# ScalarE copies placed before VectorE subtractions, two intermediates moved to PSUM, and new bookings, in a one-core decoder layer

## The chip, the cores and the metric

The kernel runs on one core of one Trainium2 chip. The metric is the device time of one execution in microseconds (us). The core has a matmul engine (TensorE, PE in the profile, with its weight loads as PEld), VectorE (DVE), ScalarE (ACT), GpSimd (POOL) and SyncE (SP), which issues nearly all DMAs here. Each engine runs its own instructions strictly in the order of the program and waits on semaphores.

## What is computed

One decoder layer on 512 tokens of width 1024, in fp32. The core of it, cut from the reference:

```python
h = rms_norm(x, n1g) * (1 + sc1) + sh1            # sc1, sh1 ... from silu(c) @ ada_w
proj = h @ w_in                                   # 1024 x 3400
y_moba = moba_attention(qm, km, vm)               # 6 heads x 64
y_conv = conformer_conv(ca, cg, ...)              # 31 taps, 256 channels, layer norm, silu
score = sum_h wi[t,h] * relu(qi[t,h] . ki[s])     # indexer; causal; 8 heads x 64
y_dsa = attention over the top 128 keys by score  # 6 heads x 64
mix = [rms_norm(y_moba), y_conv, rms_norm(y_dsa)]
x = x + g1 * (mix @ w_out)
h2 = rms_norm(x, n2g) * (1 + sc2) + sh2
y = top-1 group of 4, top-2 of its 8 experts: (silu(h2 @ w1) * (h2 @ w3)) @ w2, gated
out = rms_norm(x + g2 * y, final_g)
```

## The kernel before

The program is one long list of instructions written in an order that the Python code fixes by hand; no scheduler reorders it. It has three parts.

First (0 to about 46 us of the profiled span) the condition vector is multiplied with `ada_w`, the first norm is made, and the indexer's projections are accumulated in five PSUM banks (`pidx`).

Second (to about 355 us) come the projections, the attention and the output projection. A loop over `ORDER` (L1088) takes eleven pairs of 128-column blocks ("units") of `w_in`. Each unit is eight steps of k; a step is three products of 512 columns (high x high, high x low, low x high halves of fp32 numbers, L468 to L470, or six of 256 columns for the value units, L463 to L465). Between the steps, other work is woven in:

- `finish` (L573) takes a finished unit out of its PSUM bank. For a query unit `stacked` (L621) copies one half of the partitions on ScalarE (L624) and subtracts on VectorE (L625), then does the same for the other half. For a key unit L599 to L601 do so with two copies per half. Instructions of two engines on one PSUM bank are held apart by semaphores.
- In the first three pairs, `idx_item` (L663) makes one head's indexer score at every second step: two products (L671, L672), a relu on ScalarE into a buffer `a` of which there are four (L674), and a multiply-add into `acc` on VectorE (L675). After the eighth head `topk` books the search for the 128th score: 16 times MAX8 and MATCH_REPLACE8 and a mask (L690, L693, L696), 33 steps for each of three query tiles.
- Such background work on VectorE stands in three lists `bg`, taken in their order. `spent` (L532) adds credit for planned matmul time times `RATE` (0.5 in the first three pairs, then 0.6) and releases the next booked item when the credit covers its price. `conv_taps` books 16 taps of the convolution on VectorE (L716) for each of two channel halves; 14 more go to ScalarE and GpSimd (L727, L728), one every third step.
- `after(n, f)` runs f n steps later. `att_item` (L815) makes one pair of heads for one query tile: scores (L631, L633), minimum and mask on VectorE (L828), exponentials on ScalarE (L830); then after `lag(0)` steps the scaling (L834 to L842), after `lag(1)` the transposes and their copies (L849, L851), after `lag(2)` the product with the values (L863, copy L868, squares L872 and L874), after `lag(3)` the sum of squares as a product (L882) and, once a group of tiles is complete, the root `rsqrt` (L258 to L263, eleven VectorE steps on 128x1 to 128x4 numbers) and, `L6` steps after it, `spread` (L335), which transposes the root for use by all columns. The lags are `L1` to `L4`, and `LT` after the loop over `ORDER`.
- `ada_load` (L942) and `ada_use` (L956) multiply the rest of `ada_w` in 1 MB pieces; the first `ada_load` also clears a row buffer on GpSimd (L937), and SyncE's small DMAs into that buffer (L939) wait for it, ahead of the piece's own DMA (L948).

The loop ends with `put`, which splits the mixed rows, and 40 steps of the output projection follow, with the last four attention items among them; then four tiles are finished and routed (`Tile2`, `route`).

Third (355 us to the end) come 16 blocks of two experts each, with 1 MB weight loads, and the final norm (`final_ops`, L1823). The change touches in it only `rsqrt_ops`.

Of the kernel before, what the change touches and what calls it, by code (L numbers as in the profile page):

```python
# [34 lines left out]
NG = 2  # L35
RATE = [0.5, 0.6]
EVERY = 4.25
L1 = 4
L2 = 4
L3 = 4  # L40
L4 = 6
L5 = 3
# [39 lines left out]
L6 = 3  # L82
LT = (3, 3, 3, 4)
NF = 2
VADA = (0, 0)
ORDER = [(0, 3), (9, 11), (10, 12), (1, 4), (6, 7), (2, 5), (13, 16), (8, 19), (14, 17), (20, 21), (15, 18)]


@with_exitstack
def tile_hybrid_layer(  # L90
# [25 lines left out]
    def mk(pool, shape, dt, tag, bufs):  # L116
        cnt[0] += 1
        return pool.tile(shape, dt, tag=tag, bufs=bufs, name=f"{tag}_{cnt[0]}")
# [134 lines left out]

    def rsqrt_ops(r, v, n, shape):

        b, t = mk(sm, [P, NT], F32, "rq", 8)[:, :shape[1]], mk(sm, [P, NT], F32, "rq", 8)[:, :shape[1]]
        ri = r.bitcast(I32)
        ops = [lambda: V.tensor_scalar(b, v, 1.0 / n, EPS, op0=OP.mult, op1=OP.add),  # L258
               lambda: V.tensor_scalar(ri, b.bitcast(I32), -0.5, float(0x5f3759df), op0=OP.mult, op1=OP.add)]
        for _ in range(3):  # L260
            ops += [lambda: V.scalar_tensor_tensor(t, r, -0.5, b, op0=OP.mult, op1=OP.mult),
                    lambda: V.tensor_tensor(t, t, r, op=OP.mult),
                    lambda: V.scalar_tensor_tensor(r, t, 1.5, r, op0=OP.add, op1=OP.mult)]  # L263
        return ops

    def rsqrt(r, v, n, shape):
        for f in rsqrt_ops(r, v, n, [P, r.shape[1]]):
            f()
# [14 lines left out]
    def first_norm():  # L283
# [17 lines left out]
        A.activation(sc, col("c", 0, 8), AF.Silu)  # L301
        rsqrt(rstd, ss, D, [P, NT])
        for k in range(2, TA):
# [247 lines left out]
    def after(n, f):  # L551
        later.append([n, f])
# [20 lines left out]
    def finish(u, p):  # L573
# [10 lines left out]
        else:  # L584
# [9 lines left out]
            if i == 0:  # L594
                stacked(d, p)
            else:
                kl = (tq if (m, j) in (("m", 1), ("d", 0)) else tb)([P, T], F32R)
                for e_, own, other in HALVES:
                    A.copy(d[e_][own], p[own])  # L599
                    A.copy(d[e_][other], p[own])  # L600
                    V.tensor_tensor(kl[own], p[own], d[e_][own].bitcast(F32), op=OP.subtract)  # L601
                d = d + [kl]
            after(LQ, lambda: qkv.__setitem__((m, u - b), d))

# [16 lines left out]
    def stacked(d, p):  # L621

        for e_, own, other in HALVES:
            A.copy(d[e_][own], p[own])  # L624
            V.tensor_tensor(d[e_][other], p[own], d[e_][own].bitcast(F32), op=OP.subtract)  # L625

# [36 lines left out]
    def idx_item(qt, h):  # L663
        n = (qt + 1) * P
        if h == 0:
# [6 lines left out]
        PE.matmul(p[:, :n], q, kl[:, :n], start=False, stop=True)  # L672
        r = ta([P, T])
        A.activation(r[:, :n], p[:, :n], AF.Relu)  # L674
        V.scalar_tensor_tensor(acc[:, :n], r[:, :n], wi[:, qt - 1, h:h + 1],  # L675
                               cmask[:, 384 - qt * P:] if h == 0 else acc[:, :n],
# [5 lines left out]
    def topk(qt):  # L682
        n = (qt + 1) * P
        acc = am[qt]
        d = n / 960 + 0.07
        m8 = [None]
# [21 lines left out]
    def conv_taps(j):  # L708
# [21 lines left out]
        def f2():  # L730
            while any(e[0] == j for e in taps):
                taps.pop(0)[1]()
            V.tensor_tensor(cy[j], cy[j], cz[j], op=OP.add)
        bg[2].append((0.4, f0))
        for w in range(30 - TAPS):
            bg[2].append((0.6, lambda w=w: f1(w)))
        if TAPS:
# [77 lines left out]
    def att_item(m, qt, j):  # L815
# [61 lines left out]
        def f4(sq):  # L877
# [5 lines left out]
            for g in GROUPS[m]:  # L883
                if qt in g and done[m].issuperset(g):
                    r = mk(sm, [P, NT], F32, "r4", 3)[:, :len(g)]
                    rsqrt(r, pss[m][:, g[0]:g[-1] + 1], 384, [P, NT])
                    after(L6, lambda r=r, g=g: f5(r, g))

# [1050 lines left out]
```

## Time and profile before

| | |
|---|---|
| median of 3 runs | 862.08 us (861.08 to 864.18) |
| the profiled execution | 859.55 us |
| its span in the trace | 857.7 us |
| PE busy | 812.6 us (95%) |
| VectorE busy | 460.0 us (54%) |
| ScalarE busy | 263.8 us (31%) |
| GpSimd busy | 267.0 us (31%) |
| granted clock of TensorE, mean | 0.984 |

Busy time is the union of an engine's instructions. A matmul's end is modelled, so a PE that is busy may still run below its pace. The granted clock is a share of 2.4 GHz; 0.5 is 1.2 GHz. In a timeline row the number in square brackets is the idle time of the engine before the instruction, with the one that released it. Times inside the span are counted from its start.

### The profile page before, as it was taken

Reading aid. Unit: us, or ns where it says so; the run is one execution under the profiler, and the core shown is the slowest. Engines: PE = TensorE matmul, PEld = TensorE weight load, DVE = VectorE, ACT = ScalarE, POOL = GpSimd, SP = SyncE. Lnnn points to the kernel's source line nnn. Section 1 sums busy time; section 2 is a strip of 40 time slices with the busy share of each in tenths; the row PEclk is TensorE's granted clock in tenths of the full one; section 3 lists DMA queues with packets and bytes.
Section 4 is the critical chain, followed back from the end, with each engine's and each line's share of the span. In section 5 each row is a group of like instructions: output and inputs, shape, how many; then the busy total and the mean of one; then the engine's idle time right before and its main releaser. Section 6 shows DMA issues by size and latency. Waiting matters only on the chain.

```text
span 857.7 us, 12505 instructions
## 1 busy us (share of the span) xinstructions
PE 812.6 (95%) x4669; PEld 481.1 (56%) x4669; DVE 460.0 (54%) x1054; ACT 263.8 (31%) x573; POOL 267.0 (31%) x314
## 2 busy tenths in 40 slices
PE   6999899998999889989999999999999999999992
PEld 4888576575676678434645446346436445454431
DVE  5779989899658856573233242152333232332425
ACT  5265467645567423341110101011101001101004
POOL 1463867665413640505005013031050050050002
PEclk9999899999999999999999999999999999999997
DMA  9970554273324646679799999999999999999922
GB/s 348 335 176 1 194 171 146 81 235 109 124 99 167 250 169 276 275 289 362 280 422 419 420 418 420 419 418 420 419 421 418 420 420 418 420 419 387 375 90 101
DMA packets 76233, 252.00 MB, mean 294 GB/s; under 512 B 7575, under 2 KB 40449, under 8 KB 51082
## 3 DMA queue, kind: packets, MB, share of 16 engines
q1 hardware_dynamic: 76106, 251.15, 75.7%
q8 instruction: 38, 0.62, 0.3%
q14 instruction: 25, 0.20, 0.1%
q10 hardware_dynamic: 64, 0.02, 0.0%
HBM read 249.05 MB, written 2.10 MB: 293 GB/s over the span
## 4 chain that ended last, share of the span: by engine, by line
PE 74%; DVE 16%; ACT 3%; issue 3%; DMA 1%; POOL 1%; SPq 1%; ACTq 0%; DVEq 0%; POOLq 0%
PE ps L1488 26%; PE ps L1522 13%; PE ps L1550 7%; PE ps L1586 6%; DVE q L716 4%; DVE b L693 2%; DVE sm L690 2%; DVE b L675 2%; PE ps L468 2%; DMA ad<-in_ada_w_dram 1%; PE ps L470 1%; PE ps L469 1%; PE ps L1070 1%; PE ps L1071 1%; PE ps L1072 1%
## 5 line engine op out<-in xcount | busy, mean ns | idle before, releaser
L1570 POOL TENSOR_SCALAR v<-c,sm 128x128 bf16<-128x128 f32 x112 | 65.1, 603 | 313.4 <-DVE sm L1601 313.4
L1488 PE MATMUL ps<-u,x 128*64 128x512 f32 x280 | 103.2, 594 | 0.0
L1542 DVE TENSOR_TENSOR q<-ps,q 128x512 f32<-128x512 f32 x118 | 72.7, 683 | 40.6 <-PE ps L1550 40.6
L346 POOL TENSOR_TENSOR u<-r,u 128x512 fp32r<-128x512 f32 x55 | 76.5, 1399 | 54.0 <-ACT u L345 46.4
L1505 DVE SCALAR_TENSOR_TENSOR a<-a,sm,ps 128x512 f32<-128x512 f32 x16 | 12.0, 748 | 129.6 <-PE ps L1488 87.5
L1488 PE MATMUL ps<-h,x 128*64 128x512 f32 x248 | 78.9, 594 | 0.0
L1488 PE MATMUL ps<-r,x 128*64 128x512 f32 x240 | 78.2, 594 | 0.0
L1522 PE MATMUL ps<-u,a 128*64 128x512 f32 x200 | 70.1, 614 | 2.5 <-ACT a L1514 2.5
L1532 DVE TENSOR_TENSOR ps<-ps,q 128x512 f32<-128x512 f32 (+1 forms) x33 | 22.4, 678 | 71.7 <-PE ps L1522 71.7
L1533 ACT CAST a<-ps 128x512 fp32r<-128x512 f32 (+1 forms) x33 | 18.9, 573 | 135.2 <-DVE ps L1532 135.2
L468 PE MATMUL ps<-h,u 128*128 128x512 f32 x128 | 54.6, 427 | 0.0
L1550 PE MATMUL ps<-a,v 128*128 128x512 f32 (+1 forms) x132 | 54.3, 413 | 0.0
L1488 PEld LDWEIGHTS ps<-u,x 128*64 128x64 f32 x280 | 31.4, 137 | 37.8 <-issue 35.8
L470 PE MATMUL ps<-h,u 128*128 128x512 f32 x128 | 51.5, 402 | 0.0
L469 PE MATMUL ps<-h,u 128*128 128x512 f32 x128 | 51.3, 401 | 0.0
L1522 PE MATMUL ps<-h,a 128*64 128x512 f32 (+1 forms) x144 | 50.5, 572 | 0.6 <-DVE g L1535 0.6
L1550 PE MATMUL ps<-g,v 128*128 128x512 f32 (+1 forms) x132 | 50.8, 387 | 0.1
L1488 PEld LDWEIGHTS ps<-r,x 128*64 128x64 f32 x240 | 24.0, 137 | 38.4 <-issue 35.8
L1522 PE MATMUL ps<-r,a 128*64 128x512 f32 x120 | 43.0, 596 | 0.0
L728 POOL TENSOR_TENSOR q<-q,g 128x510 f32<-128x510 f32 (+12 forms) x26 | 36.0, 1385 | 20.3 <-ACT g L727 13.1
L1594 ACT ACTIVATE x<-ps,c,c 128x256 f32<-128x256 f32 x28 | 14.3, 560 | 90.5 <-PE ps L1586 90.5
L1497 ACT ACTIVATE a<-ps 128x512 f32<-128x512 f32 x16 | 9.6, 598 | 104.6 <-PE ps L1488 93.5
(372 smaller groups left out, 1815.4 us busy)
## 6 DMA issues: line engine op xcount, KB each, us to landing
u<-in_expert_w_dram SPq DMA_DIRECT2D x60, 1024.0 KB
r<-in_expert_w_dram SPq DMA_DIRECT2D x48, 1024.0 KB
h<-in_expert_w_dram SPq DMA_DIRECT2D x46, 1024.0 KB
z<-in_expert_w_dram SPq DMA_DIRECT2D x24, 1024.0 KB
r<-in_ada_w_dram SPq DMA_DIRECT2D x16, 1024.0 KB
r<-in_w_in_dram SPq DMA_DIRECT2D x22, 512.0 KB
ad<-in_ada_w_dram SPq DMA_DIRECT2D x8, 1024.0 KB
h<-in_expert_w_dram SPq DMA_DIRECT2D x16, 256.0 KB
```

The costliest lines, as they stand in the source:

```text
L346: eng.tensor_tensor(l, r, h.bitcast(F32), op=OP.subtract)
L468: PE.matmul(p, wh, h, start=k == 0, stop=False)
L469: PE.matmul(p, wh, l, start=False, stop=False)
L470: PE.matmul(p, wl, h, start=False, stop=k == KD - 1)
L716: V.scalar_tensor_tensor(cy[j][:, s:], cu[j][:, :T - s], col("cw", 2 * w + j), cy[j][:, s:], op0=OP.mult, op1=OP.add)
L728: G.tensor_tensor(cz[j][:, s:], cz[j][:, s:], t[:, s:], op=OP.add)
L1488: PE.matmul(self.pu[s, :], self.feature(k)[:, s], self.w[i][e][k // 4][:, k % 4, :], start=k == 0, stop=k == KD - 1)
L1522: PE.matmul(self.py[nh][s, cs], self.hT[:, k, s], self.second(e, k, nh)[:, cs], start=k == 0, stop=k == 3)
L1542: V.tensor_tensor(xr[t_, nh], self.product(yy, t_), xr[t_, nh], op=OP.add)
L1550: PE.matmul(pc[:, cs] if held else pc, self.ot[:n, t_ * P:(t_ + 1) * P], yy[q][:n, cs], start=not held and q == 0, stop=last and q == 1)
L1570: ops.append(lambda o=b.choice(ch, t_), c_=c_[:, t_:t_ + 1]: eng.tensor_scalar(o, iota, c_, None, op0=OP.is_equal))
L1586: PE.matmul(p[:, kk], hb[q][t_][i][:, k * P:k * P + P], self.o[t_ // 2][:, t_ % 2], start=t_ == 0 and q == 0, stop=t_ == NT - 1 and q == 1)
```

## The change

In `finish` and `stacked`, ScalarE's copies of a bank are all issued first, and VectorE's subtractions follow. In `idx_item` the relu is written back into the PSUM bank and VectorE reads it there. In `rsqrt_ops` the two intermediates stand in a PSUM tile (except in the first norm). The price of a search step rises by 0.13 and that of a convolution tap from 0.6 to 0.95, the second `RATE` from 0.6 to 0.8. `L4` goes from 6 to 10, `LT` from (3, 3, 3, 4) to (2, 3, 2, 3), the wait before the moba group's spread from 3 to 6 steps, the wait before the last pair's heads may be used from 6 to 4, and the last pair is projected in the order 18, 15.

```diff
--- before.py
+++ after.py
@@ -33,12 +33,12 @@
 NA = 4
 NV = 5
 NG = 2
-RATE = [0.5, 0.6]
+RATE = [0.5, 0.8]
 EVERY = 4.25
 L1 = 4
 L2 = 4
 L3 = 4
-L4 = 6
+L4 = 10
 L5 = 3
 VSOON = 0
 PUT0 = 4
@@ -80,10 +80,10 @@
 WOL = ((-2, 1, 2), (-1, 0, 0), (-1, 0, 4))
 GROUPS = {"m": ((0, 1, 2, 3),), "d": ((0,), (1, 2, 3))}
 L6 = 3
-LT = (3, 3, 3, 4)
+LT = (2, 3, 2, 3)
 NF = 2
 VADA = (0, 0)
-ORDER = [(0, 3), (9, 11), (10, 12), (1, 4), (6, 7), (2, 5), (13, 16), (8, 19), (14, 17), (20, 21), (15, 18)]
+ORDER = [(0, 3), (9, 11), (10, 12), (1, 4), (6, 7), (2, 5), (13, 16), (8, 19), (14, 17), (20, 21), (18, 15)]
 
 
 @with_exitstack
@@ -251,9 +251,11 @@
             nc.sync.dma_start(rw[:, b, 0:4], router_group_w[0, i * T:(i + 1) * T].rearrange("(p k) e -> p k e", k=4))
             nc.sync.dma_start(rw[:, b, 8:40], router_expert_w[0, i * T:(i + 1) * T].rearrange("(p k) e -> p k e", k=4))
 
-    def rsqrt_ops(r, v, n, shape):
-
-        b, t = mk(sm, [P, NT], F32, "rq", 8)[:, :shape[1]], mk(sm, [P, NT], F32, "rq", 8)[:, :shape[1]]
+    def rsqrt_ops(r, v, n, shape, apart=True):
+
+
+        w = ps([P, 2, NT]) if apart else mk(sm, [P, 2, NT], F32, "rq", 8)
+        b, t = w[:, 0, :shape[1]], w[:, 1, :shape[1]]
         ri = r.bitcast(I32)
         ops = [lambda: V.tensor_scalar(b, v, 1.0 / n, EPS, op0=OP.mult, op1=OP.add),
                lambda: V.tensor_scalar(ri, b.bitcast(I32), -0.5, float(0x5f3759df), op0=OP.mult, op1=OP.add)]
@@ -263,8 +265,8 @@
                     lambda: V.scalar_tensor_tensor(r, t, 1.5, r, op0=OP.add, op1=OP.mult)]
         return ops
 
-    def rsqrt(r, v, n, shape):
-        for f in rsqrt_ops(r, v, n, [P, r.shape[1]]):
+    def rsqrt(r, v, n, shape, apart=True):
+        for f in rsqrt_ops(r, v, n, [P, r.shape[1]], apart):
             f()
 
     def turns(*chains):
@@ -299,7 +301,7 @@
         for k in range(2):
             A.copy(xk(k), pt[k])
         A.activation(sc, col("c", 0, 8), AF.Silu)
-        rsqrt(rstd, ss, D, [P, NT])
+        rsqrt(rstd, ss, D, [P, NT], False)
         for k in range(2, TA):
             A.copy(xk(k), pt[k])
         p = spread(rstd)
@@ -598,9 +600,10 @@
                 for e_, own, other in HALVES:
                     A.copy(d[e_][own], p[own])
                     A.copy(d[e_][other], p[own])
+                for e_, own, other in HALVES:
                     V.tensor_tensor(kl[own], p[own], d[e_][own].bitcast(F32), op=OP.subtract)
                 d = d + [kl]
-            after(LQ, lambda: qkv.__setitem__((m, u - b), d))
+            after(LQ - 2 if ci == NC - 1 else LQ, lambda: qkv.__setitem__((m, u - b), d))
 
     vals = {}
 
@@ -622,6 +625,7 @@
 
         for e_, own, other in HALVES:
             A.copy(d[e_][own], p[own])
+        for e_, own, other in HALVES:
             V.tensor_tensor(d[e_][other], p[own], d[e_][own].bitcast(F32), op=OP.subtract)
 
     def product_of_pair(p, q, qs, k, kl, n):
@@ -670,9 +674,8 @@
         q = qi[h // 2][h % 2][:, qt * P:(qt + 1) * P]
         PE.matmul(p[:, :n], q, kh[:, :n], start=True, stop=False)
         PE.matmul(p[:, :n], q, kl[:, :n], start=False, stop=True)
-        r = ta([P, T])
-        A.activation(r[:, :n], p[:, :n], AF.Relu)
-        V.scalar_tensor_tensor(acc[:, :n], r[:, :n], wi[:, qt - 1, h:h + 1],
+        A.activation(p[:, :n], p[:, :n], AF.Relu)
+        V.scalar_tensor_tensor(acc[:, :n], p[:, :n], wi[:, qt - 1, h:h + 1],
                                cmask[:, 384 - qt * P:] if h == 0 else acc[:, :n],
                                op0=OP.mult, op1=OP.add)
         spent(0.11 * (qt + 1))
@@ -682,7 +685,7 @@
     def topk(qt):
         n = (qt + 1) * P
         acc = am[qt]
-        d = n / 960 + 0.07
+        d = n / 960 + 0.2
         m8 = [None]
 
         def f1():
@@ -731,9 +734,9 @@
             while any(e[0] == j for e in taps):
                 taps.pop(0)[1]()
             V.tensor_tensor(cy[j], cy[j], cz[j], op=OP.add)
-        bg[2].append((0.4, f0))
+        bg[2].append((0.7, f0))
         for w in range(30 - TAPS):
-            bg[2].append((0.6, lambda w=w: f1(w)))
+            bg[2].append((0.95, lambda w=w: f1(w)))
         if TAPS:
             for w in range(29, 29 - TAPS, -1):
                 taps.append((j, lambda w=w: g1(w)))
@@ -884,7 +887,7 @@
                 if qt in g and done[m].issuperset(g):
                     r = mk(sm, [P, NT], F32, "r4", 3)[:, :len(g)]
                     rsqrt(r, pss[m][:, g[0]:g[-1] + 1], 384, [P, NT])
-                    after(L6, lambda r=r, g=g: f5(r, g))
+                    after(L6 + 3 * (m == "m"), lambda r=r, g=g: f5(r, g))
 
         def f5(r, tiles):
             q = spread(r)
```

## Rows read from the trace of the kernel before

**Rows 1.** Windows: length; busy us of PE, PEld, DVE, ACT, POOL; clock; DMA; GB/s.
```profile
85.80:107.20 21.40, 17.44 (x68) 12.53 (x67) 20.99 (x40) 10.69 (x20) 18.48 (x13) 0.84 0.57 194
...
193.00:214.40 21.40, 18.78 (x104) 12.10 (x107) 20.20 (x38) 11.33 (x30) 11.26 (x14) 0.92 0.33 109
...
300.20:321.60 21.40, 18.12 (x77) 14.98 (x78) 12.44 (x29) 5.31 (x11) 10.64 (x9) 0.92 0.47 169
...
643.30:686.20 42.90, 42.90 (x248) 22.24 (x246) 12.46 (x23) 4.99 (x9) 0.00 (x0) 1.00 1.01 420
```

**Rows 2.** Waits of PE from 40 to 420 us: total us, times, longest.
```profile
PE ps L335 <- DVE r L263: 5.0, 2, 4.3
PE ps L978 <- DMA r<-in_ada_w_dram: 4.0, 1, 4.0
PE ps L882 <- ACT q L868: 2.6, 1, 2.6
PE ps L863 <- ACT a L851: 2.5, 2, 1.4
...
PE ps L849 <- DVE v L838: 1.7, 3, 1.1
```

**Rows 3.** Timeline, 81 to 100 us, one engine after another: start, us, instruction.
```profile
81.54 0.67 DVE L582 TENSOR_TENSOR q<-q,a 128x512 f32<-128x512 f32 x1
...
82.25 0.72 ACT L724 ACTIVATE q<-q,m 128x511 f32<-128x511 f32 x1 [3.75 <-DVE q L582]
...
92.73 0.53 POOL L937 MEMSET q<- 128x512 f32 x1
...
94.52 0.36 SPq L948 DMA_DIRECT2D r<-in_ada_w_dram  x1
...
99.94 1.93 PE L978 MATMUL ps<-r,c 128*32 128x512 f32 x8 [3.96 <-DMA r<-in_ada_w_dram]
```

**Rows 4.** The indexer's multiply-add by its line: ns minimum/median/maximum, first and last start.
```profile
L675 DVE SCALAR_TENSOR_TENSOR b<-a,m,b x21: 483/740/1742, 57.9 to 102.2; 128x256 f32<-128x256 f32 x7, 128x384 f32<-128x384 f32 x7, 128x512 f32<-128x512 f32 x7
```

**Rows 5.** Timeline, 201 to 207 us, VectorE, ScalarE and PE.
```profile
201.38 3.90 DVE L716 SCALAR_TENSOR_TENSOR q<-q,m,q 128x485 f32<-128x485 f32 x4
...
206.03 0.58 ACT L624 CAST z<-ps 64x512 fp32r<-64x512 f32 x1 [2.63 <-DVE z L625]
...
203.73 0.40 PE L469 MATMUL ps<-h,u 128*128 128x512 f32 x1
203.97 0.40 PE L470 MATMUL ps<-h,u 128*128 128x512 f32 x1
206.95 0.38 PE L882 MATMUL ps<-c,a 128*128 128x1 f32 x2 [2.58 <-ACT q L868]
```

**Rows 6.** Timeline, 164 to 167 us, ScalarE and PE.
```profile
164.76 0.58 ACT L624 CAST z<-ps 64x512 fp32r<-64x512 f32 x1 [1.46 <-DVE z L625]
...
166.80 1.25 PE L863 MATMUL ps<-a,q 128*64 128x128 f32 x12 [1.40 <-ACT a L851]
```

**Rows 7.** Timeline, 297 to 304 us, GpSimd, VectorE and PE.
```profile
297.98 2.76 POOL L1059 TENSOR_TENSOR r<-r,q 128x512 f32<-128x512 f32 x2
...
298.48 1.07 DVE L259 TENSOR_SCALAR r<-rq 128x3 int32<-128x3 int32 x1
...
301.58 1.17 DVE L263 SCALAR_TENSOR_TENSOR r<-rq,r 128x3 f32<-128x3 f32 x1
...
303.48 0.55 PE L335 MATMUL ps<-c,r 128*128 128x128 f32 x3 [4.26 <-DVE r L263]
```

**Rows 8.** A root's first step by its line, from PSUM and from SBUF: ns minimum/median/maximum.
```profile
L258 DVE TENSOR_SCALAR rq<-ps x4: 147/156/163, 230.3 to 298.3; 128x4 f32<-128x4 f32 x2, 128x1 f32<-128x1 f32 x1, 128x3 f32<-128x3 f32 x1
L258 DVE TENSOR_SCALAR rq<-sm x4: 144/147/152, 321.8 to 343.9; 128x1 f32<-128x1 f32 x4
```

**Rows 9.** Groups by line, 64 to 345 us: busy us, mean ns | idle before.
```profile
L716 DVE SCALAR_TENSOR_TENSOR q<-q,m,q 128x482 f32<-128x482 f32 (+15 forms) x32 | 33.9, 1060 | 0.8
...
L690 DVE MAX8 sm<-b 128x8 f32<-128x256 f32 (+2 forms) x48 | 26.8, 558 | 1.2
```

## The prediction, made before the result was known

> **What bounds the kernel now.** I read the windows by stage first. In the expert blocks PE is busy for the whole window at full clock, while the DMA engines are full too; the change issues nothing there, so from about 355 us on I take the time as fixed. The other three windows of [rows 1] are the places where PE falls short: 17.44 of 21.4 us with the clock at 0.84, then 18.78 and 18.12 with 0.92. VectorE is full there in the first two (20.99 and 20.20 of 21.4). So before 355 us PE is the bound, but it is stopped a few times by something slower, and each long stop is followed by a stretch at 1.2 GHz.
>
> The waits of PE name the stops [rows 2]: 4.0 us on a DMA, 2.6 on ScalarE (L882), 5.0 in two waits on the root, 2.5 in two on a ScalarE copy, 1.7 on VectorE. The clock's price comes from [rows 1]: 21.4 x 0.16 = 3.4 us behind the first, 21.4 x 0.08 = 1.7 us behind each of the other two. Of the 3.4 about 0.4 fall into the wait itself, so 3.0 are lost work. Then I followed each stop back.
>
> **The change, part by part.**
>
> *Relu in PSUM, fewer search steps early.* The DMA stop at 95.6 us begins on VectorE [rows 3]. The convolution's gating (L582) starts only at 81.54, ScalarE's first tap (L724) waits 3.75 us for it, GpSimd's splits and taps queue behind ScalarE, its clearing of the row buffer (L937) comes at 92.73, SyncE issues the piece of `ada_w` at 94.52, and PE gets it at 99.94. VectorE is late for two reasons. The indexer's multiply-add reads two SBUF tensors and takes 0.48 us at best but up to 1.74 [rows 4], the long ones while GpSimd works; and search steps of some 0.5 us (half of them MAX8 at 0.56 on average [rows 9]) are woven between. From the eighth head of the first tile to the end of the third pair there are 15 pairs of steps with some 0.83 credits each, and 1.5 held: 13.9 credits. At 0.337 a step they pay all 33 steps of the first search and six of the second; at 0.467 they pay 30. So about nine steps of 0.5 us leave this stretch, and the multiply-adds, reading PSUM, should all run near their minima. VectorE then reaches L582 some 3 to 4 us sooner (not before the sigmoid that it needs), and the clearing some 4 us sooner. The stop is 4.0 us. I count 4.0 + 3.0 = 7.0, less 0.3 that may remain: **6.7**. The bounds are 0 and 7.0. The relu's PSUM write has no row; it is off the path, since ScalarE is busy 10.69 of 21.4 us in that window [rows 1]. The bank is now held until VectorE has read it, and PE would wait if VectorE fell behind by most of the eight banks.
>
> *Copies first.* The second long stop is a chain of the ping-pong in `stacked` [rows 5]: VectorE has four taps in front (3.90 us), its subtraction of the first half comes after them, ScalarE's copy of the other half waits 2.63 us for that, and PE's L882 waits 2.58 for a ScalarE copy queued behind it. With both copies issued first ScalarE never waits for VectorE inside a unit. That is 2.6 + 1.7 = **4.3**, also covered by the four added steps of `L4`. The same shape stands at 165 us: ScalarE waits 1.46 for VectorE, PE then 1.40 for a copy behind it [rows 6]; I take **1.2** of it. What is added: VectorE's first subtraction waits for both copies (two of 0.58, four in a key unit); as VectorE is the later engine there, I cost it at nothing. If VectorE were on time it would wait up to 2 us per key unit, covered by the steps until the heads are used.
>
> *Roots in PSUM.* The third long stop is a root [rows 7]: eleven small steps, eight near 0.16 us [rows 8] and three of 1.07 to 1.18 (the first and the last are shown) while GpSimd's L1059 and L346 run; PE waits 4.26. Each step now has at most one SBUF operand. With the three at 0.16 the chain is 3 x 1.14 - 3 x 0.16 = 2.9 us shorter, which leaves 4.26 - 2.9 = 1.3 at most. In the new order this root comes five steps earlier, ahead of the router's column work that VectorE had in front of it, so between 0 and 1.3 remains; I take 0.8. Gain 4.3 - 0.8 = 3.5, and 1.7 of clock: **5.2**. The moba group's root cost the other 5.0 - 4.3 = **0.7** of that wait; it gets three more steps. A small step that writes PSUM has no row. One that reads it takes 156 ns against 147 from SBUF [rows 8], so I take 0.01 us per step more, with 0 and the contended 1.1 us as ends. Two roots have no cover, that of the last routed tile and the final one: some 35 steps, **-0.5**.
>
> [...]
>
> *Shorter lags at the end of the attention.* Counted through the loops, the last four items start two steps sooner (the last pair's wait is two shorter), and each runs through ten steps of lag rather than thirteen. A step there is three products, some 0.23 us apart [rows 5], so 0.7 us. PE already waits here: 1.1 of L863's 2.5 and most of L849's 1.7 [rows 2]. Arriving one step sooner at two of these points for four items costs between 0 and 4 x 2 x 0.7 = 5.6 us. Against it stands that the last unit is now a query unit, with two copies instead of four ahead of `put` on ScalarE. I take **-2.0**.
>
> *Later bookings.* By the same count the convolution's last tap moves from step 145 to 152 and its result, through `L4`, from 160 to 171, where the output projection needs it at about step 179. It stays in front: 0, or up to -5 if VectorE is several steps late there; I take **-0.5**. The first search ends nine steps later and the last two, all before the dsa heads use the masks. The order 18, 15 swaps two 512 KB loads of one tile, issued back to back; nothing else passes them on SyncE's queue.
>
> *VectorE's load.* Taking some 17 us of stops out leaves VectorE less time for the same work. Per microsecond of planned matmul time 0.6/0.6 = 1.0 taps are released now and 0.8/0.95 = 0.84 then, at 1.06 us each [rows 9], so its fullest stretch gets emptier by 16%. New short waits are still likely: **-1.1**, between 0 and -6.
>
> The sum: 6.7 + 4.3 + 1.2 + 5.2 + 0.7 - 0.5 - 2.0 - 0.5 - 1.1 = **14.0 us**. The profiled execution of 859.55 would become 845.5; it is 2.5 below the median of the runs shown, so the median goes from 862.08 to **848.1**.
>
> **The rivals.**
>
> *The first stop stays.* The clearing still stands behind GpSimd's splits, and the gain there needs all of 4 us. If the piece lands late by more than a little, PE waits again and the clock falls again: 848.1 + 7.0 = 855.1. For it: the sigmoid cannot come before its unit's products. Against: what GpSimd then has in front of the clearing, six pieces by the program's order, no longer meets two-SBUF multiply-adds.
>
> *The lags cost in full.* 5.6 instead of 2.0, and one more stretch at the lower clock: 848.1 + 3.6 + 1.7 = 853.4. For it: PE waits there already. Against: VectorE and ScalarE start that stretch sooner.
>
> *VectorE is the bound.* It is 94 to 98% busy in two windows of [rows 1]. Then the waits that leave ScalarE and the DMA come back on VectorE, and only the roots' 5.9 stay against 4.1 of costs: 862.08 - 1.8 = 860.3. Against: contended multiply-adds and taps are what fills it.
>
> *Small PSUM steps are slow.* Place: the final root, 24 VectorE steps after the last product, where nothing hides them, and the last routed tile's eleven. If a step that writes PSUM and is read at once by the next took as long as the contended ones, 0.95 us more, it would cost 35 x 0.95 = 33 us, and the kernel would take 881. It turns the sign from 14/35 = 0.4 us a step. For it: no row shows such a step. Against: the read from PSUM costs 0.01.
>
> **How the numbers follow.** Forecast 0.58, with its own range 842 to 855; first stop stays 0.14; lags 0.10; VectorE the bound 0.10; slow PSUM steps 0.08. About 0.3%, 2.6 us, can be told from no change. Faster: 0.56 + 0.12 + 0.10 + 0.02 = 0.80. Same: 0.02 + 0.02 + 0.06 = 0.10. Slower: 0.02 + 0.08 = 0.10. The range leaves out the slower cases (0.10), half of VectorE's case (0.05) and 0.04 below: 840 to 860.5.
>
> **What would show it.** In the profile after: no wait of L978 on a DMA near 95 us and L937 before 90; the L675 rows near 0.5 to 0.75 us; no wait of ScalarE's L624 on VectorE and none of L882 on L868; root steps all near 0.16 us and L335 waiting under 1.3; a clock of 1.00 in the windows that had 0.84 and 0.92. The prediction is wrong if a stop of several us stands elsewhere before 355, most likely at L849 or L863 in the tail, or if the expert blocks take longer than before.

## The result and the profile after

The changed kernel takes 850.32 us in the median (849.15 to 851.99), the kernel before 862.08 beside it (861.08 to 864.18); the ratio is 0.985 with an interval of 0.983 to 0.988, and the two medians differ by 11.8 us. A fourth execution of the kernel before took 1355.59 us and is left out of its median. The profiled execution takes 850.73 us, its span is 848.9. The two traces differ by only 8.8 us, because the profiled execution of before (859.55) is 2.5 us faster than its median. So the sum of 14.0, which was made against that execution, is to be held against 8.8; the median came out 2.2 us above the forecast of 848.1, inside the range of 842 to 855.

The windows of the changed kernel, with the columns of [rows 1]; the third is a stretch where the kernel before had no stop:

```profile
85.80:107.20 21.40, 21.40 (x108) 16.08 (x107) 18.35 (x44) 13.41 (x24) 18.12 (x15) 1.00 0.60 198
193.00:214.40 21.40, 21.40 (x156) 16.44 (x152) 19.18 (x36) 13.80 (x36) 11.18 (x13) 1.00 0.43 148
236.00:257.40 21.40, 17.21 (x98) 13.28 (x97) 13.93 (x42) 13.61 (x29) 0.00 (x0) 0.93 0.08 21
300.20:321.60 21.40, 20.79 (x105) 16.32 (x104) 9.95 (x25) 8.01 (x17) 12.18 (x10) 1.00 0.75 294
643.30:686.20 42.90, 42.90 (x225) 19.18 (x225) 15.98 (x29) 5.14 (x9) 4.29 (x8) 1.00 1.01 419
```

The three short windows of [rows 1] are full or nearly so, at full clock, VectorE is 1 to 2.6 us emptier in the first two, and the expert blocks are as before. The loss stands in the new row: PE busy 17.21 of 21.4, VectorE 13.93, GpSimd not at all. The waits of PE in the changed kernel, 40 to 420 us, as in [rows 2] (lines are two to three numbers higher: L866 was L863, L852 was L849, L337 was L335, L981 was L978):

```profile
PE ps L866 <- ACT a L854: 5.5, 2, 4.2
...
PE ps L852 <- DVE v L841: 1.8, 1, 1.8
PE ps L885 <- POOL a L877: 1.3, 2, 0.9
PE ps L337 <- DVE r L265: 1.0, 2, 0.8
...
PE ps L885 <- DVE ps L260: 0.9, 1, 0.9
```

The 4.0 us on a DMA, the 2.6 of L882 and 4.0 of the 5.0 on the roots are gone. One wait of 4.2 us, at L866, is new. Following the same projection products through both traces gives what each stretch gained or lost (us; the times are those of the changed kernel, the sum is of unrounded values). "Waiting" is the part that PE's waits of over 0.15 us make of it, "clock" the part that half of the time at half clock makes. What the prediction and the expectations call 1.2 GHz is a granted clock of 0.50: from 102.8 to 105.3 us of the kernel before it stands at 0.50, and products of 512 columns start 0.43 us apart, 1.2 columns a ns; from 106 to 112 us it is 1.00, and they start 0.23 apart, 2.2 columns a ns. The 2.4 GHz of full speed is an estimate from the first of these, 1.2 / 0.50.

```
stretch        gained  waiting  clock   terms of the prediction that lie in it
to 152.8         6.9      4.4    1.7    first stop 6.7
152.8 to 176.9  -1.3     -0.2   -1.7    copies first, the stop at 165 us: 1.2
176.9 to 231.3   8.2      3.9    1.7    copies first, the stop at 204 us: 4.3; moba group's root 0.7
231.3 to 257.9  -7.8     -4.2   -1.7    later bookings -0.5, VectorE's load -1.1
257.9 to 286.0  -5.2     -1.9    0.0    shorter lags -2.0
286.0 to 309.4   8.8      4.3    1.7    third stop (root) 5.2
309.4 to end    -0.9     -0.8    0.2    small PSUM steps -0.5
sum              8.8      5.5    1.9    14.0
```

What the two columns leave of a stretch is for the most part work that stands elsewhere, and neither gained nor lost. Sixteen small products (sums of squares and root transposes) lie in the third stretch of the kernel before and in the fourth of the changed one. The shorter lags and the earlier start of the last items bring 35 (28 of them products with the values) from the sixth stretch into the fifth: 3.2 of the 5.2 us lost there and 2.8 of the 8.8 gained behind are these. The first row's clock is 3.4 us behind the stop, less 1.7 at 12 us of the changed execution (0.94 in its first 30 us, against 1.00 before).

The new stop, from the timeline of ScalarE, VectorE and PE, 246 to 254 us of the changed kernel:

```profile
246.02 0.57 ACT L601 CAST b<-ps 64x512 fp32r<-64x512 f32 x1
...
247.78 0.58 ACT L602 CAST b<-ps 64x512 fp32r<-64x512 f32 x1
248.27 0.62 ACT L347 CAST u<-r 128x512 fp32r<-128x512 f32 x1
248.91 1.28 ACT L776 ACT_TABLE_LOAD   x1
251.27 1.52 ACT L776 ACTIVATE q<-q,m 128x512 f32<-128x512 f32 x2 [1.08 <-DVE q L775]
...
252.97 0.87 ACT L854 COPY a<-ps 128x384 f32<-128x384 f32 x2
...
248.40 1.39 DVE L604 TENSOR_TENSOR b<-ps,b 64x512 fp32r<-64x512 f32 x2 [1.57 <-ACT b L602]
...
250.55 1.28 DVE L775 TENSOR_TENSOR q<-q,ps 128x512 f32<-128x512 f32 x2
...
253.51 0.71 PE L866 MATMUL ps<-a,q 128*64 128x128 f32 x4 [4.18 <-ACT a L854]
```

This is the last key unit, which now comes ahead of the query unit. Its four copies run to 248.4; VectorE's two subtractions wait for all of them (1.57) and end at 249.8; only then, behind one split of weights, comes the convolution's scaling (L775), by the prediction's count eleven steps later than before, and ScalarE, which has loaded the table for the silu, stands idle 1.08 for it. The copy that PE needs (L854, `att_item`'s transposed weights) is queued behind the silu. It is neither the key nor the convolution's result that PE waits for, but a third item behind both on ScalarE.

### The profile page after: what moved, and what is told of

The parts are those of the page before. It is cut to its first block, busy times and chain, and to the rows that moved or that the text cites. A ratio compares the mean times of both kernels' runs of the same rounds, so it can differ in the third digit from the quotient of the medians.

```text
span 848.9 us, 12499 instructions
## 1 busy us (share of the span) xinstructions
PE 809.9 (95%) x4669; PEld 479.8 (57%) x4669; DVE 442.1 (52%) x1054; ACT 266.3 (31%) x573; POOL 261.9 (31%) x314
## 4 chain that ended last, share of the span: by engine, by line
PE 86%; DVE 6%; ACT 3%; POOL 2%; issue 1%; DMA 0%; ACTq 0%; POOLq 0%; DVEq 0%
PE ps L1491 26%; PE ps L1525 13%; PE ps L1553 7%; PE ps L1589 6%; PE ps L470 4%; PE ps L471 3%; PE ps L472 3%; PE ps L465 2%; PE ps L981 2%; PE ps L466 1%; PE ps L467 1%; PE ps L866 1%; PE ps L852 1%; PE ps L391 1%; PE ps L1481 1%
## 5 line engine op out<-in xcount | busy, mean ns | idle before, releaser
L348 POOL TENSOR_TENSOR u<-r,u 128x512 fp32r<-128x512 f32 x55 | 73.7, 1346 | 53.4 <-ACT u L347 42.5
L470 PE MATMUL ps<-h,u 128*128 128x512 f32 x128 | 54.0, 422 | 0.0
L471 PE MATMUL ps<-h,u 128*128 128x512 f32 x128 | 50.6, 396 | 0.0
L472 PE MATMUL ps<-h,u 128*128 128x512 f32 x128 | 50.5, 394 | 0.0
L1491 PEld LDWEIGHTS ps<-h,x 128*64 128x64 f32 x248 | 24.2, 137 | 31.1 <-issue 29.9
```

Source lines behind the costliest of these rows:

```text
L348: eng.tensor_tensor(l, r, h.bitcast(F32), op=OP.subtract)
L470: PE.matmul(p, wh, h, start=k == 0, stop=False)
L471: PE.matmul(p, wh, l, start=False, stop=False)
L472: PE.matmul(p, wl, h, start=False, stop=k == KD - 1)
L1491: PE.matmul(self.pu[s, :], self.feature(k)[:, s], self.w[i][e][k // 4][:, k % 4, :], start=k == 0, stop=k == KD - 1)
```

## Experiments

All ratios are to the kernel before, beside it on the same chip. The changed kernel's own is 0.985 (0.983 to 0.988). A difference under some 0.004 between two of them lies within the intervals. Where two kernels were timed on different chips, I compare them by these ratios.

**The relu alone on the kernel before.**

```diff
-        r = ta([P, T])
-        A.activation(r[:, :n], p[:, :n], AF.Relu)
-        V.scalar_tensor_tensor(acc[:, :n], r[:, :n], ...
+        A.activation(p[:, :n], p[:, :n], AF.Relu)
+        V.scalar_tensor_tensor(acc[:, :n], p[:, :n], ...
```

> The kernel before with the indexer's relu left in its PSUM bank and nothing else changed. Theory (the multiply-add that reads two SBUF tensors beside GpSimd made the first stop): its steps all run near 0.5 to 0.75 us, PE's wait of 4.0 us on a DMA near 96 us falls under 0.6 us and the 1.2 GHz stretch there goes, the ratio is 0.991 to 0.994. Rival (the search steps woven in make the stop too, as the prediction has it): 1 to 2.5 us of the wait stay, ratio 0.994 to 0.998. Second rival (VectorE's time goes into further search steps and stops later on): the first stop goes and a stop of 2 us or more after 120 us is new, ratio over 0.996.

856.10 us, ratio 0.992 (0.989 to 0.994). Of this kernel the group of the longest multiply-adds (busy us, mean ns), GpSimd's clearing from the timeline, and two of PE's waits, 90 to 320 us:

```profile
L674 DVE SCALAR_TENSOR_TENSOR b<-ps,m,b 128x512 f32<-128x512 f32 x7 | 5.1, 733 | 0.0
...
90.95 0.53 POOL L936 MEMSET q<- 128x512 f32 x1
...
PE ps L631 <- ACT q L867: 3.0, 1, 3.0
PE ps L881 <- ACT q L867: 2.6, 1, 2.6
```

The stop at 96 us is gone entirely, with the old prices of the search. So the theory holds for this stop, and the search steps did not have to move. Of the second rival the stop comes, though its ratio of over 0.996 does not: of the two waits, the one at L881 (202.7 us) is that of L882 in [rows 2], but of the 3.0 at L631 (217.2 us) only 0.6 was there before. Part of the gain is given back there (2.5 us of waiting), and of the 3.4 us of clock behind the first stop only some 1.7 show in the mean granted clock, 0.986 over 856.8 us against 0.984 over 857.7. The profiled execution (858.63 us) is the slowest of the four, and its trace is only 0.9 us shorter than that of before.

**The changed kernel with the relu in SBUF.** The diff above the other way round.

> The changed kernel with the relu in its SBUF buffer again. Theory (two SBUF operands are what made the multiply-add slow): its rows go back to between 0.5 and 1.7 us, VectorE is 6 to 8 us longer in the indexer's stretch, the clearing on GpSimd comes 2 us or more later and the DMA wait near 95 us returns in part, with the 1.2 GHz stretch behind it: 3 to 7 us above the changed kernel. Rival (the later search alone cures it): no DMA wait, within 1.5 us of the changed kernel.

853.38 us, ratio 0.989 (0.986 to 0.993). The multiply-adds (ns minimum/median/maximum) and the clearing in this kernel, then in the changed kernel, with the piece of `ada_w` issued behind it:

```profile
L679 DVE SCALAR_TENSOR_TENSOR b<-a,m,b x21: 483/927/1765, 56.6 to 97.4; 128x256 f32<-128x256 f32 x7, 128x384 f32<-128x384 f32 x7, 128x512 f32<-128x512 f32 x7
91.44 0.53 POOL L941 MEMSET q<- 128x512 f32 x1
```

```profile
L678 DVE SCALAR_TENSOR_TENSOR b<-ps,m,b x21: 482/608/752, 55.6 to 94.0; 128x256 f32<-128x256 f32 x7, 128x384 f32<-128x384 f32 x7, 128x512 f32<-128x512 f32 x7
88.20 0.53 POOL L940 MEMSET q<- 128x512 f32 x1
89.99 0.36 SPq L951 DMA_DIRECT2D r<-in_ada_w_dram  x1
```

PE waits 1.7 us for the piece here, against 4.0 before and nothing after. Against the forecast the clock is no lower here: the mean granted clock of the profiled execution is 0.988, against 0.986 in the changed kernel. Counted from the first product of the unit ahead of the stop (91.7 us before, 92.3 here, 93.7 with the relu alone), the clearing stands at +1.0 before, -0.8 here and -2.7 with the relu alone: earlier by 1.9 and 3.7 us, and the wait is shorter by 2.3 and 4.0. The new prices alone give somewhat over half of it, the relu alone all. The head of the chain of [rows 3], VectorE's gating, comes 2.3 us earlier here and 2.2 with the relu alone, counted in the same way, so there the two are worth alike. What the relu gains beyond that lies on GpSimd, whose pieces ahead of the clearing are no longer drawn out: one split of weights just ahead of it in the kernel before, then the same with the relu alone:

```profile
91.05 1.74 POOL L346 TENSOR_TENSOR u<-r,u 128x512 fp32r<-128x512 f32 x1
```

```profile
89.72 1.30 POOL L346 TENSOR_TENSOR u<-r,u 128x512 fp32r<-128x512 f32 x1
```

So in this stretch the multiply-add that reads two SBUF tensors goes with a slower GpSimd (1.74 us in place of 1.30 for the split) as well as being slower itself (up to 1.77 us, against 0.75 from PSUM).

**Copies first, alone on the kernel before.** Both places are edited alike (L599 and L624); one is shown.

```diff
         for e_, own, other in HALVES:
             A.copy(d[e_][own], p[own])
+        for e_, own, other in HALVES:
             V.tensor_tensor(d[e_][other], p[own], ...
```

> The kernel before with one edit: ScalarE's copies of a bank first, then VectorE's subtractions. Theory (the ping-pong on one bank is what stops PE at 204 us): ScalarE's waits for VectorE at the unit copies, 16.5 us in all before, go to under 2, L882's wait of 2.6 us and the 1.2 GHz stretch behind it go, the wait at 165 us shrinks; the DMA wait near 95 us stays at 3 us or more. Time 5 to 6 us below the kernel before. Rival (the order of copies only moves the waiting to VectorE, and the lags do the work): within 1.5 us of the kernel before, with a stop of 2 us or more still near 204 us.

854.44 us, ratio 0.989 (0.986 to 0.993). Two of PE's waits, 90 to 320 us:

```profile
PE ps L335 <- DVE r L263: 5.0, 2, 4.3
PE ps L980 <- ACT u L345: 3.7, 1, 3.7
```

The wait of L882 is gone, and with it ScalarE's waits for VectorE at the unit copies; the roots stand as they were, and the first stop too, though it now ends on a ScalarE copy. By the medians the edit gains 9.7 us, by the two traces 4.9 (spans 857.7 and 852.8). That 4.9 lies near the estimate of 5.5 is in part chance. Around 204 us 3.7 are gained, but 1.7 are given back at 215 us, where PE waits 1.3 for a small copy behind a key unit's four; and 1.4 come from a shorter slow stretch behind the first stop (a granted clock of 0.92 from 85.8 to 107.2 us, against 0.84), which itself is only 0.3 shorter.

**The changed kernel with the old order of copies.** The diff above the other way round.

> The changed kernel with the old order of copies and subtractions. Theory: ScalarE waits for VectorE between the halves again, 10 us or more in all; longer L4 covers the stop at 204 us, but other waits of PE behind ScalarE copies come back: 2 to 5 us above the changed kernel. Rival (lags and bookings do it): within 1.5 us of the changed kernel; the stop near 249 us, where VectorE waits 1.6 us for four copies, would even be shorter.

854.01 us, ratio 0.989 (0.985 to 0.992). The sum of squares does not wait near 204 us here either, so another part of the change, most likely the longer `L4`, covers that stop as well. What comes back is smaller: 1.2 us at 210 us, at L633, behind a key unit between whose halves ScalarE waits 0.75 for VectorE; with the prediction's 1.7 of clock behind a stop, an estimate here, 2.9 us in all. The waits on L854's copies, 5.5 us in the changed kernel, sum to 8.7; 2.4 of them are the chain of [rows 6] at 161 us. What the edit is worth is thus some 3 us when all else is changed, hardly more than the intervals, and 5 to 10 alone.

**The changed kernel with the old price of a search step.**

```diff
-        d = n / 960 + 0.2
+        d = n / 960 + 0.07
```

> The changed kernel with the old price of a search step (n/960 + 0.07). Theory: about nine more steps, 4 to 5 us of VectorE, stand ahead of the convolution's gating, so the clearing comes later and a DMA wait of 0 to 3 us returns; the convolution ends earlier by about the credits saved, so the stop near 249 us shrinks: between 3 us above and 4 us below the changed kernel. Rival (the relu alone cures the first stop): no DMA wait, and below the changed kernel by up to 6 us through the earlier convolution.

860.23 us, ratio 0.995 (0.994 to 0.997), the most that any single edit cost: 8.5 us more than the changed kernel. The first stop does not come back, so of the rival that half holds; both forecasts of the time fail. Waits of PE, 100 to 230 us, and ScalarE's queue ahead of the longest:

```profile
PE ps L635 <- ACT q L871: 4.1, 1, 4.1
PE ps L852 <- DVE v L841: 3.7, 4, 1.6
PE ps L852 <- POOL v L845: 1.4, 2, 1.2
...
220.61 0.56 ACT L601 CAST z<-ps 64x512 fp32r<-64x512 f32 x1
...
222.37 0.58 ACT L602 CAST z<-ps 64x512 fp32r<-64x512 f32 x1
222.97 0.27 ACT L871 COPY q<-ps 128x128 f32<-128x128 f32 x1
```

At the rate of 0.8 the cheap search steps fill VectorE (41.1 of 42.8 us busy between 107 and 150 us, against 39.2 in the changed kernel), and the waits at L852 lie between 120 and 169 us. The 4.1 us at 223 has the same shape as the stop at 249: four copies of a key unit in front of a small copy that PE needs. There VectorE was idle.

**The changed kernel with all old bookings** (rate, both prices of the convolution, price of the search).

```diff
-RATE = [0.5, 0.8]
+RATE = [0.5, 0.6]
-        d = n / 960 + 0.2
+        d = n / 960 + 0.07
-        bg[2].append((0.7, f0))
+        bg[2].append((0.4, f0))
-            bg[2].append((0.95, lambda w=w: f1(w)))
+            bg[2].append((0.6, lambda w=w: f1(w)))
```

> The changed kernel with all the old bookings of VectorE's background work (rate 0.6; 0.4 and 0.6 for the convolution, 0.07 for a search step), the rest as changed. Theory (what cost 8.7 us with the old search price alone was VectorE filled too full by the old price at the new rate): VectorE is about as full as before the change, waits of 1 to 4 us between 120 and 225 us are half as many as there, the stop at 249 us goes because the convolution is done some ten steps earlier, ratio 0.980 to 0.986. Rival (the old price alone is what hurts, at either rate): stops of 1 to 4 us between 120 and 225 us as there, ratio 0.990 to 0.997.

851.27 us, ratio 0.988 (0.985 to 0.990). The rival falls: it is the old price at the new rate that hurts. Of the theory half holds. There are stops at 210 and 225 us (1.3 and 2.3 us, both on ScalarE), and the stop at 249 shrinks to 1.9 us but does not go. All the bookings together are worth some 2 us or nothing.

**Convolution's scaling after six steps again; the old order of the last pair; both.**

```diff
-            after(L4, lambda: f2(sq[0]))
+            after(6, lambda: f2(sq[0]))
```

```diff
-ORDER = [..., (20, 21), (18, 15)]
+ORDER = [..., (20, 21), (15, 18)]
```

> The changed kernel, in which only the step from the convolution's last tap to its scaling and silu runs after six steps, as before the change, and no longer after ten. In the trace of the changed kernel that scaling (250.55 us) and the silu behind it (251.27, 1.52 us) stand between the key unit's four copies on ScalarE and the copy that PE waits 4.18 us for at 249 us; with the 1.2 GHz stretch behind it the stop takes some 6 us. Theory (the later booking made this stop): four steps earlier, some 6 us, the silu is done before the key unit; the stop shrinks below 1 us, the 1.2 GHz stretch of 254 to 258 us goes, the ratio to the kernel before falls from 0.985 to 0.978 to 0.981. Rival (VectorE is late there whatever the order, by its filled queue): the stop stays at 3 us or more, at this place or up to 10 us from it, ratio 0.983 to 0.987. Second rival (the stop is only deferred to the tail): the stop goes, but waits of 270 to 290 us grow by as much, ratio 0.983 to 0.986.

> The changed kernel with the last pair of units in the old order, query unit 15 ahead of key unit 18. Theory (the stop at 249 us comes from the key unit's four copies and two subtractions standing ahead of the convolution's silu): with the query unit there the silu comes some 1 us sooner and the stop falls from 4.2 to 2.5 to 3.5 us, but the key unit's four copies then stand ahead of the last items and waits of 255 to 275 us grow by 1 to 2 us; ratio to the kernel before 0.983 to 0.988. Rival (the order of the two units decides the stop): the stop and the 1.2 GHz stretch go, ratio 0.978 to 0.981. Second rival (the key is needed soonest): PE waits over 4 us for the key further on and the ratio is over 0.990.

> The changed kernel with both edits that shrank the stop at 249 us one at a time: the convolution's scaling after six steps instead of ten, and the last pair of units in the old order. Theory (two jobs on ScalarE add up ahead of the copy that PE waits for, the silu with its table load and wait, 3.9 us, and the two copies that a key unit has more than a query unit, 1.2 us): with both away the stop falls from 4.2 us (2.6 and 3.2 with one edit each) to under 1 us, no 1.2 GHz stretch follows, and the ratio to the kernel before goes from 0.9829 and 0.982 to 0.977 to 0.981. Rival (the key unit's four copies only move on to the next item): a wait of 1.5 us or more appears between 255 and 275 us, ratio 0.981 to 0.985.

848.05 us, ratio 0.983 (0.980 to 0.985), with the first; 847.89 us, 0.982 (0.980 to 0.985), with the second; 846.76 us, 0.983 (0.980 to 0.985), with both. PE's L866 at the stop, in this order:

```profile
252.58 1.25 PE L866 MATMUL ps<-a,q 128*64 128x128 f32 x12 [2.47 <-ACT a L854]
```

```profile
251.80 1.25 PE L866 MATMUL ps<-a,q 128*64 128x128 f32 x12 [3.00 <-ACT a L854]
```

```profile
250.76 1.25 PE L866 MATMUL ps<-a,q 128*64 128x128 f32 x12 [1.40 <-ACT a L854]
```

From 4.2 the wait falls to 2.5, 3.0 and 1.4: the two edits take 1.7 and 1.2, and together 2.8. So the stop is the sum of two jobs on ScalarE, as expected, and the larger part is the convolution's, moved by the later bookings and by `L4`. The forecast for the old order (2.5 to 3.5 us) came true, but the two of under 1 us failed: with both edits a table load of 1.28 us, the exponentials and the unit's two copies still stand ahead. The times gain 2 to 3 us by the ratios, and with both edits no more than with one; in the profiled executions the mean granted clock is 0.988 with both, against 0.992 and 0.990 with one, which is 3.4 and 1.7 us of some 846. Each of the three is about 0.003 below the changed kernel, but the intervals overlap, so that a faster kernel is likely and not shown.

**The changed kernel with the old lags at the end of the attention.**

```diff
-LT = (2, 3, 2, 3)
+LT = (3, 3, 3, 4)
```

> The changed kernel with the old lags of the attention's last items (3, 3, 3 and 4 steps in place of 2, 3, 2 and 3). The changed kernel loses some 3 to 5 us between 258 and 286 us against the kernel before, in six waits of PE of 0.6 to 1.3 us on ScalarE, VectorE and GpSimd. Theory (shorter lags made these waits): most of them fall under 0.6 us and the ratio to the kernel before goes from 0.985 to 0.981 to 0.983. Rival (the lags buy something that the waits cost): the last items end later, the root behind them comes later and PE waits for it again, 1 to 4 us; ratio 0.985 to 0.990. The stop at 249 us is the same in both.

853.76 us (848.54 to 855.24), ratio 0.987 (0.983 to 0.991). ScalarE and PE, 284 to 287 us:

```profile
285.62 0.62 ACT L347 CAST z<-r 128x512 fp32r<-128x512 f32 x1 [3.41 <-POOL r L1062]
286.14 1.07 ACT L854 COPY a<-ps 128x512 f32<-128x512 f32 x2
...
286.77 2.46 PE L866 MATMUL ps<-a,q 128*64 128x128 f32 x16 [1.97 <-ACT a L854]
```

Up to 286 us of the changed kernel this one gains 4.1 against it. Of these 1.8 are waits, as the theory says; the rest is 21 small products that stand further on here. Then it loses more than that again, 5.9 by 309 us, 2.2 of it waits and 1.7 clock. The last item's copy now falls behind a cast (L347) for which ScalarE stands 3.41 us waiting for GpSimd, PE waits 2.0, and its sixteen products behind the wait take 2.46 us, where sixteen take 1.09 in the changed kernel (284.02). So the rival's ratio comes true, but not its mechanism: no wait for a root is among them. The wait is moved, not saved; the shorter lags cost nothing that this measurement can tell.

**One of the four lags longer, on the kernel with both edits.** `LT = (2, 3, 3, 3)`.

> The same with one lag of the last items longer by one step, from the transposes to the products with the values (2, 3, 3, 3 in place of 2, 3, 2, 3). Theory (that lag alone makes the wait of 1.5 to 1.7 us for a ScalarE copy near 272 us): that wait falls under 0.6 us, the others stay, ratio 0.001 to 0.002 below the kernel with the first two edits. Rival (ScalarE's queue decides: with all four lags longer a copy stood behind a cast that waited 3.4 us for GpSimd, and PE waited 2.0 us for it at 287 us): such a wait of 1 us or more takes its place, ratio equal or up to 0.004 higher.

846.56 us, ratio 0.982 (0.980 to 0.984): the same as without it. The wait near 272 us falls from 1.5 to 0.8, and two waits on GpSimd's sum of squares (L877) grow to 1.8 and 1.3. Which of the lags would help stays open.

**The changed kernel with the roots' intermediates in SBUF.**

```diff
-        w = ps([P, 2, NT]) if apart else mk(sm, [P, 2, NT], F32, "rq", 8)
+        w = mk(sm, [P, 2, NT], F32, "rq", 8)
```

> The changed kernel with the intermediates of all the reciprocal roots in SBUF again. Theory (VectorE's small steps with two SBUF inputs take 1.1 in place of 0.16 us while GpSimd works): some steps near 300 us take 1 us or more again, PE waits 2 to 4 us there and falls to 1.2 GHz, the ratio to the kernel before goes from 0.985 to 0.990 to 0.993; the roots without cover (the last routed tile's and the final one) cost the same in both, within 0.5 us. Rival (the root came earlier by the new order alone, so PSUM did nothing): PE's wait for the root stays under 0.6 us and the ratio within 0.003 of 0.985. Second rival (small steps in PSUM are slower): uncovered roots are faster here, the end from the last product on is 1 to 2 us shorter than in the changed kernel.

855.00 us, ratio 0.991 (0.988 to 0.994), 4.4 us more than the changed kernel by the ratios. The root of the first dsa tile in this kernel, VectorE, GpSimd and PE, 282 to 287 us, and then the same root in the changed kernel:

```profile
282.56 1.09 DVE L263 SCALAR_TENSOR_TENSOR rq<-r,rq 128x1 f32<-128x1 f32 x1
...
284.63 1.19 DVE L264 TENSOR_TENSOR rq<-rq,r 128x1 f32<-128x1 f32 x1
...
282.36 1.28 POOL L1082 TENSOR_TENSOR q<-v,q 128x512 f32<-128x512 f32 x1 [2.06 <-DVE rq L260]
...
286.74 0.45 PE L337 MATMUL ps<-c,r 128*128 128x128 f32 x1 [3.10 <-DVE r L265]
```

```profile
281.69 1.28 POOL L1082 TENSOR_TENSOR q<-v,q 128x512 f32<-128x512 f32 x1 [2.06 <-DVE ps L260]
...
281.91 0.17 DVE L263 SCALAR_TENSOR_TENSOR ps<-r,ps 128x1 f32<-128x1 f32 x1
...
283.80 0.29 PE L337 MATMUL ps<-c,r 128*128 128x128 f32 x1 [0.81 <-DVE r L265]
```

The step of 1.09 us starts 0.2 after GpSimd's product; with an operand in PSUM the same step takes 0.17 beside the same GpSimd work, and PE waits 0.81 instead of 3.10. So the theory's slow steps and its ratio come true, and the new order alone does not save this root.

But it is not the root of [rows 7]. That one has 128x3 numbers, of the other three dsa tiles, and stands 11 us further on. One of its steps and the products that use it in this kernel, then these products in the changed kernel:

```profile
293.76 0.16 DVE L263 SCALAR_TENSOR_TENSOR rq<-r,rq 128x3 f32<-128x3 f32 x1
...
295.63 0.51 PE L337 MATMUL ps<-c,r 128*128 128x128 f32 x3
```

```profile
291.22 0.51 PE L337 MATMUL ps<-c,r 128*128 128x128 f32 x3 [0.16 <-DVE r L265]
```

All eleven of its steps take 0.16 to 0.17 us with the intermediates in SBUF, GpSimd does nothing beside them (its last product ahead of them ends at 292.8 us), and PE does not wait for it. For the root whose 4.26 us the prediction counted, the first rival therefore holds in this kernel: the rest of the change was enough. In the changed kernel a product of GpSimd (288.4 to 289.7 us) lies beside the first steps of that root, so PSUM may help there as well; that is not shown. No run has the roots' tile alone on the kernel before.

## Why the prediction was right, and where not

**First stop, 6.7: right.** 6.8 us are gained there. The clearing starts at 88.20 (forecast: before 90), the multiply-adds lie between 0.48 and 0.75 us as forecast, and no wait of L981 on a DMA is left. One reason was superfluous: the search steps need not leave the stretch, since the relu alone removes the stop. The rival of a late piece came true, and in part, only where the relu was taken back.

**Copies first, 4.3 and 1.2: the first right, the second wrong.** The stop at 204 us is gone in every kernel with the edit, though in the changed kernel it does not come back without the edit either. Of the 8.2 us gained in the stretch 4.3 are this stop (2.6 and 1.7 of clock), 0.6 and 0.7 are two small waits of the kernel before (220 and 235 us), and the rest is mostly the sixteen products that now come later. The 1.2 at 165 us were not gained: the chain of [rows 6], which costs 2.4 with the old order of copies, is gone, but in its place L852 waits 1.8 us for VectorE at 161 us, behind search steps, with a slow stretch (0.93 from 152.8 to 176.9 us), and 1.3 are lost. That is the new wait which the term of VectorE's load held in reserve.

**Roots, 5.2: near in size, the cause in part another.** The stop of 4.26 us and its clock are gone, and the stretch gained 6.0 by waiting and clock. That a step beside GpSimd takes 0.17 us with an operand in PSUM and 1.09 without is shown, and undoing the edit costs 4.4 us by the ratios. But they are lost at the root of the first tile, which the prediction did not count; the root that it counted, which now comes earlier, ran at full pace without PSUM. The 0.81 that remains, against a forecast of 0.8, is also the first tile's; for the other 0.16 remain. That the two numbers meet is luck. This stretch and the one ahead of it together, between which products were only moved, gave 3.6, against 3.2 forecast (5.2 and -2.0).

**Small PSUM steps, -0.5: too much.** The 22 steps of the final root, where nothing hides them, first and last in the changed kernel:

```profile
836.13 0.16 DVE L260 TENSOR_SCALAR ps<-c 128x1 f32<-128x1 f32 x1
...
838.98 0.16 DVE L265 SCALAR_TENSOR_TENSOR c<-ps,c 128x3 f32<-128x3 f32 x1
```

2.85 us from the first start to the last, against 2.81 (840.67 to 843.48) for the same steps in the kernel with the roots in SBUF. That is 0.04 us for 22 steps of which 20 read PSUM, some 2 ns each, where the prediction took 10. So the rival of 881 us falls.

**Shorter lags, -2.0: right in size, but not a price of the lags.** The tail's waits grew by 1.9 us, 0.8 of them the wait for the first tile's root; the rest of its 5.2 are products moved into it. With the old lags 1.8 us of these waits go, but 2.2 come back a few steps on, and 1.7 of clock. Costing the added waits without asking what else the items would meet later was the error.

**Later bookings, -0.5: the step that failed.** The prediction counted that the convolution's result is needed at step 179 and comes at 171, and took it as hidden. The result is in time. But its silu passes through ScalarE's queue, and the new place lies just behind a key unit's four copies, with PE's copy behind both. That is 4.2 us of wait and a slow stretch (0.57 from 254 to 258 us, 1.7 us), some 6 us in place of 0.5, and about the whole distance between 14.0 and the 8.8 of the traces; the bound of -5 was named for another mechanism (a late VectorE). Moving the silu back gained 1.7 us of the wait, exchanging the two units 1.2, both 2.8; the old bookings alone took 2.3. The prediction counted the last pair's new order as a gain ("two copies instead of four ahead of `put`") and did not ask where the four went.

**The sign of being wrong came.** The prediction named as such a stop of several us elsewhere before 355 us, "most likely at L849 or L863 in the tail". The 4.2 us at L866 (L863 before) is that stop, at 249 us, just ahead of the tail; a smaller one of 1.8 us stands at L852 (L849 before). So the forecast time was met although one part of the mechanism failed.

## What to carry to other kernels

The slack of a step that is moved is not only the distance to its reader: at its new place, list on each engine that it passes what is queued behind it, and who waits for that. On the chains of small VectorE steps here, one operand in PSUM in place of two in SBUF cost 0.04 us over the 22 steps of the final root, and a step beside GpSimd's work took 0.17 us in place of 1.09. When traces are compared stretch by stretch, count what was only moved: here 3.2 of 5.2 us "lost" were products that had come forward. The gains of single edits don't add up (relu alone 5.8 us by the medians, copies alone 9.7, everything together 11.8): PE, once freed, met the next late engine, 3.0 us at L631 with the one, 1.3 at L633 with the other.

## What was not expected of the hardware

The same wait was followed by a slow clock in one execution and not in another. The stop at 161 us has the same length in two executions (1.76 and 1.77 us of L852 on VectorE), once in the changed kernel and once in that with the old order of the last pair, whose programs are the same up to there. The 5.7 us from the end of the wait:

```profile
160.90:166.60 5.70, 5.30 (x23) 2.72 (x24) 5.45 (x10) 2.30 (x4) 5.70 (x6) 0.70 0.12 19
```

```profile
161.90:167.60 5.70, 5.27 (x36) 3.64 (x36) 5.52 (x10) 3.63 (x7) 5.70 (x6) 1.00 0.16 24
```

The granted clock is 0.70 in the one, 3.4 us of it at half clock, and 1.00 in the other; 36 instructions are done in place of 23, and PE is 1.5 us further on by the next unit. So 1.7 us of clock behind a stop, as the prediction took it, is the right size (5.7 x 0.30) but not certain. It is likely a part of why single executions of one kernel differ by several us (with the old lags 848.54 us at a mean granted clock of 0.990, 855.24 at 0.980), and why a comparison of two traces, such as 8.8 us here, can be some us off the medians' 11.8.
